# Sampled-state loads one group ahead, one gate tile forward, another tile order and new task delays in a hybrid decoder trunk

## The chip, the cores and the metric

The kernel runs on one core of one Trainium2 chip. TensorE (PE) multiplies, VectorE (DVE), ScalarE (ACT) and GpSimd (POOL) work element by element, and SyncE (SP) issues the transfers between the chip's memory and the core. The metric is the device time of one execution in microseconds (us), lower is better.

## The reference

One inference step of a trunk with two layers, for 512 prompt tokens (one new sequence) and 8 sampled sequences of 4 tokens each: 544 tokens in all, model width 1024. Layer 0 is a gated delta rule (GDN, 8 heads of 128), layer 1 a Mamba-2 scan (SSD, 32 heads of 64 in 4 groups, state size 128); each is followed by a SwiGLU FFN of width 2816, and every sublayer stands between two RMS norms. Of the SSD mixer, which most of the change touches:

```python
z, xBC, dt = jnp.split(h @ w_in, [SSD_DI, SSD_DI + SSD_CONV_DIM], axis=-1)
xBC, conv_new = causal_conv(xBC, conv0, conv_w, conv_b)
xs, Bm, Cm = jnp.split(jax.nn.silu(xBC), [SSD_DI, SSD_DI + SSD_GROUPS * SSD_DSTATE], axis=-1)
dt = jax.nn.softplus(dt + dt_bias)
y, hN = ssd_chunked(xs, dt, A, Bm, Cm, h0)     # h0: each sampled sequence's state
y = rms_norm((y + D_skip[:, None] * xs) * jax.nn.silu(z), norm_w)
return y @ w_out, hN, conv_new
```

In `ssd_chunked` each group multiplies its C by the state h0 of the sequence (`y_off`). In GDN the gate z enters at the end: the normed output of the delta rule is multiplied by silu(z), and the product goes through `gdn_w_out`.

## The kernel before

All data is feature-major: 128 features on the partitions, tokens along the row, in two halves of 272 tokens (hf 0 and 1). A weight block of 128 x 512 is loaded by SP (`wr`, 256 KB), split by ACT into a rounded high part (`wh`, L242) and by DVE into the rest (`wl`, L243), and for each 128 x 128 piece three matmuls are issued: high data by high weight (L279), low data by high weight (L280), high data by low weight (L281), each over 272 columns. The program has 11008 of these weight matmuls in its stages GDN mixer, GDN output projection, FFN 0, SSD mixer, SSD output projection, FFN 1. A place in the program is given below as @n: after the n-th weight matmul.

Everything else is done by small tasks, Python generators that a clock interleaves with the weight tiles (`Flow`, from L88). The clock counts one for each product of a weight piece. A task yields `(cost, delay)` or a condition, and is taken up again when the clock has gone on by the delay. The constants at the top (`D_...`, `PACE`, `NEWTON`, `TILE`, `FACTOR`) are such delays: `D_FIN` and `NEWTON` stand ahead of the two matmuls (`ms`, `r`) of a layer norm, `D_QT` ahead of the work on a tile of q, `PACE` between the state updates (`su`) that run beside the FFNs, `D_WT` ahead of the task that makes the decay matrices `W`. So the delays decide behind which weight matmul a small matmul stands. Each engine then works through its own queue in order; SP's is one queue for all loads and stores, and a DMA there waits until its buffer is free and until an earlier DMA on the same of eight semaphores has ended. What is behind it waits too.

The order of the tiles is written out. `ORDER` (L41) names the tiles of the GDN mixer, for each head k, q, v and z. In the SSD mixer a loop builds the order (L1681 to L1692): the dt tile, `NZ` gate tiles, B and C of group 0, then 16 x tiles, with B and C of the next group after every fourth, and from x3 on a gate tile behind each. `FINE` and `WIDE` say how many of the first tiles are emitted piece by piece and how many may use the larger set of PSUM banks. `T_S` is the number of tiles of the SSD output projection that are done for half 0 first and come again for half 1.

For each SSD group `c_task` (L1476) multiplies C and B (`cb`), then the states of the eight sampled sequences (`yos <- h0T, cm`, L1508, two at a time, b0 to b7), copies the sum from PSUM (L1514), transposes it (`yoT`, L1518). The states come as `h0T`, 256 KB each, in four buffers: b0 to b3 are loaded when the group's task starts, and b4 to b7 each when the matmul that read its buffer is through. `yos` on the SBUF side takes a buffer of the same four. A 128 x 32 by 128 x 512 matmul stands as two instructions in the trace, and one to four of them on different columns of the array take about the time of one.

The x tiles' task transposes x (`xtok`), multiplies the decay matrices W, which DVE makes from a broadcast row `ar` (loaded from memory, 272 KB) and CB, by x (`yd`), and makes the new state `hT`, which SP stores (`s_hp_out`).

Of the kernel before, what the change touches and what calls it, by code (L numbers as in the profile page):

```python
# [5 lines left out]
F32 = mybir.dt.float32  # L6
# [20 lines left out]
NL = 5  # L27
KEPT = 4
HELD = 3
NZ = 2  # L30
ZLAG = 3
SLEAD = 3
FINE = 12
WIDE = 4
NH0 = 4
PACE = 5.0
LIVE = 3
RAWW = 3 + SEQ + NB * 7

ORDER = ("k0 k1 z0 q0 q1 z1 k2 k3 v0 v1 z2 q2 q3 k4 k5 v2 v3 q4 q5 k6 k7 v4 v5 q6 q7 v6 v7 "  # L40
         "z3 z4 z5 z6 z7")  # L41
GLEAD = 3
FREE_G = (True, False)
FREE_S = (False, False)
NEWTON = 2.5
TILE = 1.0
FACTOR = 5.0
D_FIN = 2.5
D_DEC0 = 8.0
D_DEC1 = 3.5  # L50
D_DEC = 3.5
D_KT = 3.5
D_QT = 11.0
D_VT = 2.5
D_ON = 3.0
D_XT = 6.0
D_WT = 16.0
D_GT = 2.0
D_INV = 1.0
D_MG = 3.0  # L60
D_S1 = 0.8
D_S2 = 1.2
D_X3 = 3.0
# [1 line left out]
D_B0 = 0.0  # L65
T_G = 5
T_F = 4
T_S = 4
BIG = 1.0e30


# [45 lines left out]
def _program(nc, tc, io, es):  # L117
# [7 lines left out]
    act = pool("act", 6)  # L125
# [6 lines left out]
    def dma(out, in_):  # L132
        nc.sync.dma_start(out=out, in_=in_)
# [188 lines left out]
    def emit(u, fine=False, wide=False):  # L322
# [107 lines left out]
    class Pre:  # L430
# [18 lines left out]
        def end(self):  # L449
            if self.free:  # L450

                st.ready[self.hf] = True
                yield 0.0, FACTOR
            y = rsq(self.ss.sum(), 1e-6)
            yield 0.0, NEWTON
            r = spread(y)
            st.ready[self.hf] = True
            if self.free:
                st.r[self.hf] = sqp.tile([P, H2], F32, tag="sq", name="r", bufs=NSQ)
                S.activation(out=st.r[self.hf], in_=r, func=AF.Copy)  # L460
# [21 lines left out]
    class Post:  # L482


        def __init__(self, kind, layer, fw, e=1e-6, extra=None):
            self.kind, self.layer, self.fw, self.e, self.extra = kind, layer, fw, e, extra
            self.ss = [None, None]
            st.ready = [False, False]

        def tile(self, m):  # L490
            def done(hf, ps):
                if self.ss[hf] is None:
                    self.ss[hf] = Squares()
# [160 lines left out]
    def gdn():  # L654
# [697 lines left out]
    def ssd():  # L1352
# [118 lines left out]
        def c_after(m, Y):  # L1471
# [2 lines left out]
            S.activation(out=g.C, in_=Y, func=AF.Silu)  # L1474
            flow.start(c_task(m - 20), 6.0)

        def c_task(gi):
            g = gp[gi]
            h0 = []

            def load(n):
                for b in range(len(h0), min(n, NB)):
                    h0.append(big.tile([P, 512], F32, tag="h0T", name="h0T", bufs=NH0))
                    dma(h0[b], io["s_h0T"][b, :, 512 * gi:512 * gi + 512])
# [80 lines left out]
        def x_task(m, xf):  # L1565
# [107 lines left out]
        tiles += [zt(m) for m in range(NZ)] + [bt(0), ct(0)]  # L1673
        xs = {}
        z = NZ
        for m in range(16):
            tiles.append(xt_(m))
            xs[id(tiles[-1][0])] = m
            if m % 4 == 2 and m < 12:
                tiles += [bt(m // 4 + 1), ct(m // 4 + 1)]  # L1680
            if m >= ZLAG:  # L1681
                tiles.append(zt(z))
                z += 1
        tiles += [zt(m) for m in range(z, 16)]
        for i, u in enumerate(units(start_first(tiles, xop, SLEAD))):
# [12 lines left out]
        conv.close("s")
# [129 lines left out]
```

## Time and profile before

| | us |
|---|---|
| median of 3 runs | 1754.37 |
| the runs | 1745.22 to 1757.28 |
| the profiled execution | 1746.99 |
| its span in the trace | 1745.2 |
| TensorE busy | 1680.0 (96%) |
| VectorE busy | 1177.2 (67%) |
| ScalarE busy | 820.0 (47%) |
| GpSimd busy | 116.1 (7%) |

The profiled execution is 1.8 us longer than its span, and 7.4 us below the median. The mean granted clock of TensorE is 0.988 of its full 2.4 GHz. A row of the timeline gives start and duration of one instruction or of several of one kind in a row, the engine, the line, what it writes and reads, and behind it in brackets how long its engine stood idle before it and what ended that. Durations of matmuls overlap, so the time of a matmul is the distance from its start to the next start.

### The profile page before, as it was taken

Reading aid. Unit: us, or ns where it says so; the run is one execution under the profiler, and the core shown is the slowest. Engines: PE = TensorE matmul, PEld = TensorE weight load, DVE = VectorE, ACT = ScalarE, POOL = GpSimd, SP = SyncE. Lnnn points to the kernel's source line nnn. Section 1 sums busy time; section 2 is a strip of 40 time slices with the busy share of each in tenths; the row PEclk is TensorE's granted clock in tenths of the full one; section 3 lists DMA queues with packets and bytes.
Section 4 is the critical chain, followed back from the end, with each engine's and each line's share of the span. In section 5 each row is a group of like instructions: output and inputs, shape, how many; then the busy total and the mean of one; then the engine's idle time right before and its main releaser. Section 6 shows DMA issues by size and latency. Waiting matters only on the chain. (4 is left out here: it accounts for less than half of the span.)

```text
span 1745.2 us, 37143 instructions
## 1 busy us (share of the span) xinstructions
PE 1680.0 (96%) x14127; PEld 1597.6 (92%) x14127; DVE 1177.2 (67%) x3103; ACT 820.0 (47%) x1813; POOL 116.1 (7%) x335
## 2 busy tenths in 40 slices
PE   6899999999999999999699999999999999999997
PEld 5888888899999999999687899999999999999996
DVE  6886868567846665336877887878469766665356
ACT  5664644447433333335465565657456433333252
POOL 1212121100000000000001110100000000000000
PEclk8999999999999999999899999999999999999998
DMA  6333323335224443235544544432445644444464
GB/s 175 103 91 86 106 68 99 101 114 177 80 74 146 139 136 95 77 108 164 189 111 126 170 142 141 131 107 66 145 153 165 194 146 139 139 146 133 129 177 127
DMA packets 164563, 223.23 MB, mean 128 GB/s; under 512 B 53344, under 2 KB 66464, under 8 KB 163872
## 3 DMA queue, kind: packets, MB, share of 16 engines
q1 hardware_dynamic: 164384, 220.85, 41.9%
q8 instruction: 111, 1.82, 0.4%
q14 instruction: 68, 0.56, 0.1%
HBM read 199.75 MB, written 21.04 MB: 127 GB/s over the span
## 5 line engine op out<-in xcount | busy, mean ns | idle before, releaser
L279 PE MATMUL mm<-xh,wh 128*128 128x272 f32 x2496 | 735.7, 295 | 6.6 <-ACT og L1175 2.3
L280 PE MATMUL mm<-xl,wh 128*128 128x272 f32 x2496 | 727.7, 292 | 0.1
L281 PE MATMUL mm<-xh,wl 128*128 128x272 f32 x2496 | 727.1, 292 | 0.0
L242 ACT ACTIVATE wh<-wr 128x512 fp32r<-128x512 f32 x558 | 345.1, 622 | 408.3 <-PE mm L280 352.6
L243 DVE TENSOR_TENSOR wl<-wr,wh 128x512 fp32r<-128x512 f32 x558 | 376.5, 679 | 222.7 <-ACT wh L242 209.9
L279 PEld LDWEIGHTS mm<-xh,wh 128*128 128x128 f32 x2496 | 473.1, 190 | 23.9 <-issue 9.9
L280 PEld LDWEIGHTS mm<-xl,wh 128*128 128x128 f32 x2496 | 472.9, 190 | 4.7 <-issue 1.2
L281 PEld LDWEIGHTS mm<-xh,wl 128*128 128x128 f32 x2496 | 471.9, 189 | 4.8 <-issue 3.7
L279 PE MATMUL mm<-gb,wh 128*128 128x272 f32 x544 | 157.7, 291 | 0.0
L281 PE MATMUL mm<-gb,wl 128*128 128x272 f32 x544 | 155.5, 288 | 1.6 <-DVE wl L243 1.6
L280 PE MATMUL mm<-gb,wh 128*128 128x272 f32 x544 | 155.4, 288 | 0.0
L616 DVE SCALAR_TENSOR_TENSOR conv<-raw,cw,conv 128x512 f32<-128x512 f32 x144 | 107.0, 743 | 16.0 <-ACT conv L612 9.3
L281 PEld LDWEIGHTS mm<-gb,wl 128*128 128x128 f32 x544 | 101.8, 188 | 2.1 <-DVE wl L243 1.8
L279 PEld LDWEIGHTS mm<-gb,wh 128*128 128x128 f32 x544 | 102.2, 188 | 1.0 <-ACT wh L242 0.2
L280 PEld LDWEIGHTS mm<-gb,wh 128*128 128x128 f32 x544 | 102.3, 189 | 0.4
L1281 ACT ACTIVATE sg<-sg 128x272 f32<-128x272 f32 x88 | 37.6, 431 | 103.6 <-DVE sg L1280 103.3
L511 POOL TENSOR_TENSOR x<-x,fw 128x272 f32<-128x272 f32 x16 | 15.4, 964 | 1022.6 <-DVE fw L509 515.9
L280 PE MATMUL mm<-yl,wh 128*128 128x272 f32 x256 | 74.3, 291 | 1.2 <-DVE yl L359 1.2
L1289 DVE TENSOR_TENSOR sg<-sg,mm 128x272 f32<-128x272 f32 x88 | 38.4, 437 | 54.6 <-PE mm L281 54.3
L281 PE MATMUL mm<-yh,wl 128*128 128x272 f32 x256 | 73.9, 291 | 1.1 <-DVE wl L243 1.1
L279 PE MATMUL mm<-yh,wh 128*128 128x272 f32 x256 | 74.0, 290 | 0.0
L424 DVE TENSOR_TENSOR acc<-acc,sq 128x272 f32<-128x272 f32 x112 | 50.5, 454 | 33.2 <-ACT sq L417 32.6
(412 smaller groups left out, 2567.0 us busy)
## 6 DMA issues: line engine op xcount, KB each, us to landing
wr<-f_d_in SPq DMA_DIRECT2D x120, 256.0 KB
wr<-f_g_in SPq DMA_DIRECT2D x98, 256.0 KB
wr<-f_u_in SPq DMA_DIRECT2D x98, 256.0 KB
wr<-g_w_in SPq DMA_DIRECT2D x68, 256.0 KB
wr<-s_w_in SPq DMA_DIRECT2D x48, 256.0 KB
wr<-s_wo_in SPq DMA_DIRECT2D x48, 256.0 KB
wr<-s_wz_in SPq DMA_DIRECT2D x36, 256.0 KB
ar<-ad SPq DMA_DIRECT2D x32, 272.0 KB
```

The lines of the kernel that those rows point to most:

```text
L242: S.activation(out=hi, in_=src, func=AF.Copy)
L243: V.tensor_tensor(out=lo, in0=src, in1=hi.bitcast(F32), op=ALU.subtract)
L279: PE.matmul(ps, lhsT=h[:, k, :], rhs=ah(k0 + k), start=first and k == 0, stop=False)
L280: PE.matmul(ps, lhsT=h[:, k, :], rhs=al(k0 + k), start=False, stop=False)
L281: PE.matmul(ps, lhsT=lo[:, k, :], rhs=ah(k0 + k), start=False, stop=last and k == n - 1)
L424: V.tensor_tensor(out=self.acc, in0=self.acc, in1=self.late.pop(0), op=ALU.add)
L511: E.tensor_tensor(out=x[:, k, :], in0=x[:, k, :], in1=f, op=ALU.add)
L616: V.scalar_tensor_tensor(out=Y[:, 0:SEQ], in0=R[:, j:j + SEQ], scalar=w[:, j:j + 1], in1=Y[:, 0:SEQ], op0=ALU.mult, op1=ALU.add)
L1281: S.activation(out=t, in_=t, func=AF.Silu)
L1289: V.tensor_tensor(out=t, in0=t, in1=ps, op=ALU.mult)
```

## The change

1. SSD's tile order is written out as `SORDER`. z3 moves from behind x4 to behind x5, z4 from behind x5 to behind x7, z5 from in front of x7 to behind it, z6 and z7 come behind x8, z8 and z9 behind x9; z2 and everything from z10 on keep their places.
2. `c_task` loads a state b+5 behind the yield that follows b, no longer right behind its matmul, and at its end loads the first four states of the next group. The SBUF copy of `yos` leaves the four state buffers for a pool of 128 x 544 tiles, so the four are states alone.
3. The task of an x tile waits also for the group's `yo` (the transposed state product).
4. In GDN's `ORDER` z3 moves from behind v7 to behind q3.
5. Delays: `PACE` 5 to 6, `D_QT` 11 to 9.5, `D_DEC1` 3.5 to 2; `NEWTON`, `FACTOR`, `D_FIN` by stage; `FINE` 12 to 24, `WIDE` 4 to 8; `T_S` 4 to 5, by which four more blocks of the SSD output projection are loaded and split a second time (45 loads, before 41).
6. `emit_together` is new, but the tuples that would call it (`KO_G`, `KO_S`) are empty. Two `og` tiles are taken from their pool earlier in the loop.

```diff
-NZ = 2
-ZLAG = 3
-FINE = 12
-WIDE = 4
+FINE = 24
+WIDE = 8
-PACE = 5.0
+PACE = 6
...
-ORDER = ("k0 k1 z0 q0 q1 z1 k2 k3 v0 v1 z2 q2 q3 k4 k5 v2 v3 q4 q5 k6 k7 v4 v5 q6 q7 v6 v7 "
-         "z3 z4 z5 z6 z7")
+ORDER = ("k0 k1 z0 q0 q1 z1 k2 k3 v0 v1 z2 q2 q3 z3 k4 k5 v2 v3 q4 q5 k6 k7 v4 v5 q6 q7 v6 "
+         "v7 z4 z5 z6 z7")
+
+SORDER = ("z0 z1 B0 C0 x0 x1 x2 B1 C1 x3 z2 x4 x5 z3 x6 B2 C2 x7 z4 z5 x8 z6 z7 x9 z8 z9 "
+         "x10 B3 C3 x11 z10 x12 z11 x13 z12 x14 z13 x15 z14 z15")
...
-NEWTON = 2.5
-TILE = 1.0
-FACTOR = 5.0
-D_FIN = 2.5
+NEWTON = (2.5, 2.5, 1.5, 2.5, 3.2)
+TILE = (1.0, 1.0, 1.0, 1.0, 1.0)
+FACTOR = (5.0, 5.0, 5.0, 4, 5.0)
+D_FIN = (2.5, 2.5, 2.5, 2.5, 3.5)
...
-D_DEC1 = 3.5
+D_DEC1 = 2
...
-D_QT = 11.0
+D_QT = 9.5
...
-T_S = 4
+T_S = 5
...
+        def load_h0(gi, n):
+            h0 = gp[gi].h0
+            for b in range(len(h0), min(n, NB)):
+                h0.append(big.tile([P, 512], F32, tag="h0T", name="h0T", bufs=NH0))
+                dma(h0[b], io["s_h0T"][b, :, 512 * gi:512 * gi + 512])
+            return h0
...
-            load(NH0)
+            h0 = load_h0(gi, NH0)
...
-                    load(b + 1 + NH0)
                     if q % 2 and b < NB - 1:
-                        yield 1.7, 1.5
-            yo = big.tile([P, 512], F32, tag="h0T", name="yos", bufs=NH0)
+                        yield 1.7, D_Y
+
+                        load_h0(gi, b + 1 + NH0)
+            yo = t544("yos")[:, 0:512]
...
+            if gi < 3:
+                load_h0(gi + 1, NH0)
             yield 0.5, 0.5
...
-            yield lambda: hasattr(d, "w")
+            yield lambda: hasattr(d, "w") and hasattr(g, "yo")
```

The order on SP about the second half of group 0's states, before: the load of b4, one of b5, then b6 and b7, and further down, behind a store and several loads, the first four of group 1.

```order
L133 DMA h0T<-s_h0T_in 128x512
L133 DMA ar<-ad 128x544
L133 DMA h0T<-s_h0T_in 128x512
L133 DMA ar<-ad 128x544
L133 DMA ep<-ead 64x544
L133 DMA h0T<-s_h0T_in 128x512 x2
L133 DMA ep<-ead 64x544
L133 DMA wr<-s_w_in 128x512
L133 DMA wr<-s_wz_in 128x512
L133 DMA ar<-ad 128x544 x2
L133 DMA ep<-ead 64x544
L133 DMA s_hp_out<-hT 128x128
```

In the changed kernel, the same place:

```order
L137 DMA ar<-ad 128x544 x2
L137 DMA ep<-ead 64x544
L137 DMA h0T<-s_h0T_in 128x512 x2
L137 DMA ar<-ad 128x544
L137 DMA ep<-ead 64x544
L137 DMA h0T<-s_h0T_in 128x512
L137 DMA s_hp_out<-hT 128x128
L137 DMA h0T<-s_h0T_in 128x512 x2
L137 DMA ar<-ad 128x544
L137 DMA ep<-ead 64x544 x2
L137 DMA h0T<-s_h0T_in 128x512 x3
L137 DMA ar<-ad 128x544
```

b4 and b5 stand together, b6 alone, the store of `hT` now stands ahead of b7, and the four loads of group 1 (the one behind b7 and the row of three) follow at once, between the loads `ar` and `ep` of the x tiles.

The order on PE about group 1's states, before: one matmul on b4, the transposes of an x tile, one on b5; twelve weight matmuls earlier stand b0 to b3 in one row, and 24 later b6 and b7.

```order
L1508 MATMUL yos<-h0T,cm 32x512
L1571 MATMUL xtok<-cst,xf 128x128 x4
L1573 MATMUL xsm<-cst,xf 32x128
L1508 MATMUL yos<-h0T,cm 32x512
L279 MATMUL mm<-xh,wh 128x272
```

In the changed kernel b0 and b1 stand between the transposes and b2 and b3 behind them; twelve weight matmuls on follow b4 and b5, and b6 and b7 come behind the x tile's products, with no weight matmul between.

```order
L1615 MATMUL xtok<-cst,xf 128x128 x2
L1549 MATMUL yos<-h0T,cm 32x512 x2
L1615 MATMUL xtok<-cst,xf 128x128 x2
L1617 MATMUL xsm<-cst,xf 32x128
L1549 MATMUL yos<-h0T,cm 32x512 x2
L284 MATMUL mm<-xh,wh 128x272
```

```order
L1638 MATMUL su<-xw,Bt 128x128 x4
L1549 MATMUL yos<-h0T,cm 32x512 x2
L1661 MATMUL yd<-W,xt 64x128 x8
L1664 MATMUL yo<-W,xts 64x32 x2
L1666 MATMUL yo<-Cf,hT 128x128 x3
L1549 MATMUL yos<-h0T,cm 32x512 x2
L284 MATMUL mm<-xh,wh 128x272
```

The order on DVE in the square root that ends GDN's delta rule (`nx` to `ny`, then `dg`, which `r` on PE waits for). Before, three splits `kl` of FFN weights stand between its first steps:

```order
L368 TENSOR_SCALAR nx<-os 68x16
L243 TENSOR_TENSOR kl<-wr,kh 128x512
L369 TENSOR_SCALAR ny<-nx 68x16
L371 TENSOR_SCALAR nh<-nx 68x16
L243 TENSOR_TENSOR kl<-wr,kh 128x512
L372 TENSOR_TENSOR nt<-ny 68x16
L243 TENSOR_TENSOR kl<-wr,kh 128x512
L373 TENSOR_TENSOR nt<-nt,nx 68x16
```

In the changed kernel two of them stand ahead of it and one inside:

```order
L248 TENSOR_TENSOR kl<-wr,kh 128x512
L1170 TENSOR_TENSOR oar<-oss,qs_4652 128x272
L248 TENSOR_TENSOR kl<-wr,kh 128x512
L401 TENSOR_SCALAR nx<-os 68x16
L248 TENSOR_TENSOR kl<-wr,kh 128x512
L402 TENSOR_SCALAR ny<-nx 68x16
L404 TENSOR_SCALAR nh<-nx 68x16
L405 TENSOR_TENSOR nt<-ny 68x16
```

On PE the matmul `os` that this root waits for stands at @1587 before and at @1599 in the changed kernel, and `r`, which waits for the root, at @1624 in both.

## Rows read from the trace of the kernel before

**Rows 1.** The page, busy time by engine, and the three costliest groups of instructions (busy us, mean ns of one, idle time before and what ended most of it).

```profile
PE 1680.0 (96%) x14127; PEld 1597.6 (92%) x14127; DVE 1177.2 (67%) x3103; ACT 820.0 (47%) x1813; POOL 116.1 (7%) x335
...
L279 PE MATMUL mm<-xh,wh 128*128 128x272 f32 x2496 | 735.7, 295 | 6.6 <-ACT og L1175 2.3
L280 PE MATMUL mm<-xl,wh 128*128 128x272 f32 x2496 | 727.7, 292 | 0.1
```

**Rows 2.** What PE waited for over the whole span: us in total, times, longest.

```profile
PE ms L396 <- DVE acc L424: 11.9, 5, 8.4
PE r L388 <- DVE dg L385: 10.4, 6, 3.5
PE mm L288 <- DVE whl L243: 8.6, 1, 8.6
PE yos L1508 <- DMA h0T<-s_h0T_in: 3.8, 2, 2.1
PE mm L281 <- DVE wl L243: 2.7, 3, 1.6
...
PE c L1394 <- ACT Ac L1446: 1.4, 1, 1.4
PE mm L280 <- DVE yl L359: 1.2, 1, 1.2
```

**Rows 3.** The timeline of PE about group 0's states (start us, duration us).

```profile
913.12 0.29 PE L280 MATMUL mm<-xl,wh 128*128 128x272 f32 x1
913.24 0.29 PE L281 MATMUL mm<-xh,wl 128*128 128x272 f32 x1
913.46 1.05 PE L1508 MATMUL yos<-h0T,cm 128*32 128x512 f32 x4
914.44 1.16 PE L1594 MATMUL su<-xw,Bt 128*128 128x128 f32 x8
915.53 1.86 PE L1508 MATMUL yos<-h0T,cm 128*32 128x512 f32 x4
917.32 0.39 PE L279 MATMUL mm<-xh,wh 128*128 128x272 f32 x1
917.55 0.29 PE L280 MATMUL mm<-xl,wh 128*128 128x272 f32 x1
...
920.71 1.04 PE L1508 MATMUL yos<-h0T,cm 128*32 128x512 f32 x2 [1.75 <-DMA h0T<-s_h0T_in]
```

**Rows 4.** The same stretch, loads of PE's stationary operand: the wait inside the row that starts at 915.53.

```profile
916.34 0.14 PEld L1508 LDWEIGHTS yos<-h0T,cm 128*32 128x32 f32 x2 [0.68 <-DMA h0T<-s_h0T_in]
```

**Rows 5.** The timeline of PE about group 1's states.

```profile
967.45 1.06 PE L1508 MATMUL yos<-h0T,cm 128*32 128x512 f32 x8
972.29 1.04 PE L1508 MATMUL yos<-h0T,cm 128*32 128x512 f32 x2 [2.06 <-DMA h0T<-s_h0T_in]
```

**Rows 6.** Busy time by stretches of 1 us: PE, PEld, DVE, ACT, POOL, each with its instructions, then the granted clock of PE, the busy share of the DMA engines and GB/s.

```profile
922.00:923.00 1.00, 1.00 (x7) 0.75 (x6) 0.00 (x0) 0.00 (x0) 0.19 (x1) 0.59 0.74 236
923.00:924.00 1.00, 1.00 (x3) 0.14 (x2) 0.00 (x0) 0.00 (x0) 0.00 (x0) 0.50 0.52 188
924.00:925.00 1.00, 1.00 (x3) 0.20 (x2) 0.00 (x0) 0.09 (x1) 0.00 (x0) 0.50 0.86 244
925.00:926.00 1.00, 1.00 (x6) 1.00 (x7) 0.00 (x0) 1.00 (x2) 0.00 (x0) 0.70 0.96 246
...
973.00:974.00 1.00, 1.00 (x5) 0.73 (x5) 0.00 (x0) 0.00 (x0) 0.00 (x0) 0.69 0.78 277
974.00:975.00 1.00, 1.00 (x4) 0.23 (x3) 0.30 (x2) 0.60 (x1) 0.00 (x0) 0.50 0.96 227
975.00:976.00 1.00, 1.00 (x2) 0.00 (x0) 0.90 (x3) 0.00 (x0) 0.00 (x0) 0.50 0.77 230
976.00:977.00 1.00, 1.00 (x4) 0.70 (x4) 1.00 (x7) 0.00 (x0) 0.00 (x0) 0.60 0.95 313
```

**Rows 7.** The same view in a stretch of 5 us.

```profile
915.00:920.00 5.00, 3.97 (x21) 2.11 (x19) 4.59 (x15) 0.28 (x1) 0.34 (x2) 1.00 1.02 271
```

**Rows 8.** The timeline of SP: when the DMAs were issued.

```profile
910.70 0.38 SPq L133 DMA_DIRECT2D h0T<-s_h0T_in  x1
...
914.53 0.80 SPq L133 DMA_DIRECT2D h0T<-s_h0T_in  x2
...
921.61 0.34 SPq L133 DMA_DIRECT2D s_hp_out<-hT  x1
...
968.53 1.28 SPq L133 DMA_DIRECT2D h0T<-s_h0T_in  x3
```

**Rows 9.** The timeline of DVE behind group 0's states: decay matrices from `ar`, the idle time, and the first product of W and CB.

```profile
915.41 0.87 DVE L1544 TENSOR_SCALAR W<-ar,sGm 128x128 f32<-128x128 f32 x4 [1.47 <-DMA ar<-ad]
...
927.78 0.69 DVE L1577 TENSOR_TENSOR xw<-xtok,coef 128x512 f32<-128x512 f32 x1 [6.20 <-ACT xt L1575]
...
932.27 0.72 DVE L1553 TENSOR_TENSOR W<-W,CB 128x544 f32<-128x544 f32 x1
```

**Rows 10.** The end of GDN's delta rule, PE.

```profile
380.98 0.60 PE L1140 MATMUL os<-cst,oar 128*68 128x4 f32 x8
386.19 2.00 PE L388 MATMUL r<-dg,cst 68*128 68x272 f32 x8
```

**Rows 11.** The same, DVE.

```profile
381.62 0.17 DVE L368 TENSOR_SCALAR nx<-os 68x16 f32<-68x16 f32 x1
381.73 0.69 DVE L243 TENSOR_TENSOR kl<-wr,kh 128x512 fp32r<-128x512 f32 x1
...
385.21 1.49 DVE L385 TENSOR_TENSOR dg<-cst,ny 68x272 f32<-68x272 f32 x4
```

More of the change, by code (lines that the diff above doesn't have):

```diff
@@ L29 @@
 HELD = 3
-NZ = 2
-ZLAG = 3
 SLEAD = 3
-FINE = 12
-WIDE = 4
+FINE = 24
+WIDE = 8
 NH0 = 4
-PACE = 5.0
+PACE = 6
 LIVE = 3
 RAWW = 3 + SEQ + NB * 7
-ORDER = ("k0 k1 z0 q0 q1 z1 k2 k3 v0 v1 z2 q2 q3 k4 k5 v2 v3 q4 q5 k6 k7 v4 v5 q6 q7 v6 v7 "
-         "z3 z4 z5 z6 z7")
+ORDER = ("k0 k1 z0 q0 q1 z1 k2 k3 v0 v1 z2 q2 q3 z3 k4 k5 v2 v3 q4 q5 k6 k7 v4 v5 q6 q7 v6 "
+         "v7 z4 z5 z6 z7")
+SORDER = ("z0 z1 B0 C0 x0 x1 x2 B1 C1 x3 z2 x4 x5 z3 x6 B2 C2 x7 z4 z5 x8 z6 z7 x9 z8 z9 "
+         "x10 B3 C3 x11 z10 x12 z11 x13 z12 x14 z13 x15 z14 z15")
+KO_G = ()
+D_Y = 1.5
+KO_S = ()
 GLEAD = 3
@@ L44 @@
 FREE_S = (False, False)
-NEWTON = 2.5
-TILE = 1.0
-FACTOR = 5.0
-D_FIN = 2.5
+NEWTON = (2.5, 2.5, 1.5, 2.5, 3.2)
+TILE = (1.0, 1.0, 1.0, 1.0, 1.0)
+FACTOR = (5.0, 5.0, 5.0, 4, 5.0)
+D_FIN = (2.5, 2.5, 2.5, 2.5, 3.5)
 D_DEC0 = 8.0
-D_DEC1 = 3.5
+D_DEC1 = 2
 D_DEC = 3.5
 D_KT = 3.5
-D_QT = 11.0
+D_QT = 9.5
 D_VT = 2.5
-D_ON = 3.0
+D_ON = 3
 D_XT = 6.0
-D_WT = 16.0
+D_WT = 16
 D_GT = 2.0
-D_INV = 1.0
-D_MG = 3.0
+D_INV = 1
+D_MG = 3
 D_S1 = 0.8
@@ L211, in _program @@
     st.free = [False, False]
+    st.stage = 0
     st.held = [[], []]
@@ L347, in emit, with emit_together @@
         flow.product(us * (s.shape[1] if fine else k0))
+    def emit_together(us, wide=False):
+        for u in us:
+            fetch_to(u[4] + len(pieces(u[0])))
+        hf = us[0][1]
+        ah, al = us[0][2](hf)
+        banks = [mmt(wide) for _ in us]
+        for k in range(KD):
+            for (srcs, _, _, _, base, kept), ps in zip(us, banks):
+                one, end = k == 0, k == KD - 1
+                if srcs[0].shape[2] < P:
+                    w = ready[base][0]
+                    PE.matmul(ps[0:64], lhsT=w[:, k, :], rhs=ah(k), start=one, stop=False)
+                    PE.matmul(ps[0:64], lhsT=w[:, k, :], rhs=al(k), start=False, stop=end)
+                    continue
+                h, lo = ready[base + k // 4]
+                j = k % 4
+                PE.matmul(ps, lhsT=h[:, j, :], rhs=ah(k), start=one, stop=False)
+                PE.matmul(ps, lhsT=h[:, j, :], rhs=al(k), start=False, stop=False)
+                PE.matmul(ps, lhsT=lo[:, j, :], rhs=ah(k), start=False, stop=end)
+            flow.product(1.0)
+        for u, ps in zip(us, banks):
+            if st.free[hf] and st.r[hf] is None:
+                st.held[hf].append((u[3], ps))
+            else:
+                u[3](hf, ps)
+            flow.pump()
     def stack(tile, src, first):
@@ L452, in end @@
                 st.ready[self.hf] = True
-                yield 0.0, FACTOR
+                yield 0.0, FACTOR[st.stage]
             y = rsq(self.ss.sum(), 1e-6)
-            yield 0.0, NEWTON
+            yield 0.0, NEWTON[st.stage]
             r = spread(y)
@@ L488, in __init__ @@
             st.ready = [False, False]
+            st.stage += 1
         def tile(self, m):
@@ L497, in done @@
                 if self.ss[hf].n == KD:
-                    flow.start(self.finish(hf), D_FIN)
+                    flow.start(self.finish(hf), D_FIN[st.stage])
             return done
@@ L502, in finish @@
             y = rsq(self.ss[hf].sum(), self.e, None if self.extra is None else self.extra[:, half(hf)])
-            yield 0.0, NEWTON
+            yield 0.0, NEWTON[st.stage]
             r = spread(y)
@@ L512, in finish @@
                 pre.square(k)
-                yield 0.0, TILE
+                yield 0.0, TILE[st.stage]
             yield from pre.end()
@@ L1207, in gdn @@
             n = names.get(id(u[0]))
-            if i == 1:
+            if i == 1 or (i == 0 and 0 in KO_G):
                 load_small()
+            if i == 2:
+                og += [act.tile([P, 4, T], F32, tag="x", name="og") for _ in range(2)]
             if i == 2 * GLEAD - 1:
@@ L1213, in gdn @@
                 load_zeros()
-                og += [act.tile([P, 4, T], F32, tag="x", name="og") for _ in range(2)]
             if n is not None and u[1] == 0 and i >= GLEAD and n[0] == "k":
@@ L1220, in gdn @@
                     flow.start(decay(h // 2 + 1), D_DEC)
+            if i % GLEAD < 3 and i < 2 * GLEAD and i // GLEAD in KO_G:
+                if i % GLEAD == 0:
+                    emit_together(us[i:i + 3])
+                continue
             emit(u)
@@ L1451, in ssd @@
         pr = [State() for _ in range(16)]
+        for g in gp:
+            g.h0 = []
         def b_after(m, Y):
@@ L1475, in c_after @@
             flow.start(c_task(m - 20), 6.0)
+        def load_h0(gi, n):
[4 more added lines that the diff above has]
+            return h0
         def c_task(gi):
             g = gp[gi]
[L1479 to L1484, printed above, removed]
-            load(NH0)
+            h0 = load_h0(gi, NH0)
             ps = dbank("cb")
@@ L1672, in ssd @@
         zt = lambda m: ([io["s_wz"][m]], z_done(m))
-        tiles += [zt(m) for m in range(NZ)] + [bt(0), ct(0)]
         xs = {}
[L1675 to L1685, printed above, removed]
+        for n in SORDER.split():
+            i = int(n[1:])
+            tiles.append({"x": xt_, "z": zt, "B": bt, "C": ct}[n[0]](i))
+            if n[0] == "x":
+                xs[id(tiles[-1][0])] = i
+        us = units(start_first(tiles, xop, SLEAD))
+        for i, u in enumerate(us):
             flow.until(lambda: st.ready[u[1]])
@@ L1695, in ssd @@
                     flow.start(w_task(m + 2), D_WT)
+            if i < 2 * SLEAD and i % SLEAD < 3 and i // SLEAD in KO_S:
+                if i % SLEAD == 0:
+                    emit_together(us[i:i + 3], True)
+                continue
             emit(u, i < FINE, i < WIDE)
```

## The prediction

> **What bounds the kernel now.** I began with the page: TensorE is busy for 1680.0 of 1745.2 us, and nearly all of it is the three weight matmuls of a piece [rows 1]. A busy PE with spare time on every other engine leaves three things to gain: the 65 us in which PE is idle, the time in which it is busy at half clock, and small matmuls in between. The change keeps the number of weight matmuls and of small ones, so only these three can move. Next I read what ended PE's idle time [rows 2]. The largest entries, `ms`, `r` and `whl`, are the start of the program, the end of it and the norms between layers. I compared the order of both kernels there: where FFN 0 passes into SSD, at the longest wait of 8.4 us, PE and DVE have the same instructions in the same order up to the `r` that ends it, so this stays. What the change does touch is the entry `yos <- h0T`, 3.8 us in two waits.
>
> The timelines show what these cost. In group 0 PE waits 1.75 us at 920.71 for the state b6 [rows 3]; inside the row that starts at 915.53 there is a third wait, 0.68 us, for b5 [rows 4]. In group 1 it waits 2.06 us at 972.29 for b4 [rows 5]. The view by microseconds shows a second cost that no list of waits has: behind either wait the granted clock falls from the upper level (2.4 GHz) to the lower (1.2 GHz). What is missing from full clock between 922 and 926 is 0.41 + 0.50 + 0.50 + 0.30 = 1.71 us, between 973 and 977 it is 0.31 + 0.50 + 0.50 + 0.40 = 1.71 us [rows 6]. So group 0's late loads cost 0.68 + 1.75 + 1.71 = 4.14 us and group 1's 2.06 + 1.71 = 3.77 us, together 7.9 us. That is the most that the loads can give.
>
> **The loads, step by step.** b5 was issued at 910.70 and landed at 916.34, after 5.6 us; b6 was issued at 914.53 and used at 920.71, after 6.2 us; group 1's b4 was issued at 968.53 and used at 972.29, after 3.8 us [rows 3 to 5, 8]. I take 3.8 to 6.2 us for a load in this stretch.
>
> Group 0: by the orders, the matmul that frees b6's buffer moves ahead, from @5440 to @5428, and its use back, from @5451 to @5463. Between stand 35 weight matmuls, at 0.125 us from start to start (913.12 to 913.24 [rows 3]) 4.4 us, a `su` of 1.1 us and the `yos` of b4 and b5 with 1.0 us [rows 3], in all 6.5 us and some tenths for the passages between shapes. Two short DMAs go ahead of b6 on SP, about 1 us. So b6 waits between 0 and 0.7 us. b7 now stands behind the store of `hT` on SP. That store was issued at 921.61 [rows 8], far too late, but in the new order the `su` that it needs stands 8 weight matmuls earlier, and on DVE no weight split and no convolution is left between it and `hT`; I work out 916.7 on the old clock. b7 would land between 921 and 923 and is used near 922: a wait of 0 to 1.3 us. Of 4.14 us I leave 0.7 us, gain 3.4 us.
>
> Group 1: its b0 to b3 are now loaded near 917 to 922 and used some 45 us later, no question. Its b4 and b5 are still loaded after b0 and b1 were used, the change doesn't prefetch those. From there to their use are the rest of the transposes, one `yos`, twelve weight matmuls and a `su`: 0.5 + 1.0 + 1.5 + 1.1 us and passages, 4.1 to 4.5 us, against 3.8 us for the load of that very place. A wait of 0 to 0.5 us (up to 2.0 if 6.2 us held here). I leave 0.4 us, gain 3.4 us.
>
> Together the loads give 6.8 us of 7.9; the other end, nothing, is a rival below.
>
> [...]
>
> **Passages between shapes.** From a weight matmul to a small one and back costs 0.22 - 0.125 at the way in (913.24 to 913.46) and 0.23 - 0.125 at the way out (917.32 to 917.55), 0.2 us [rows 3]. Counting runs of small matmuls in both orders, GDN has 153 instead of 157 and SSD 68 instead of 77: with the others 12 fewer. Bounds 0 (a passage between two small shapes costs as much) and 2.4 us; I take 1.2 us.
>
> **z3 in GDN's tail.** One tile, 48 weight matmuls, 6.1 us, no longer covers the end of the delta rule. There `os` starts at 380.98 and `r` at 386.19 [rows 10], with 37 weight matmuls between, and the root on DVE takes 3.6 us from `nx` to `dg` [rows 11]. Now 25 lie between, 3.2 us. But two of three weight splits, 0.69 us each [rows 11], stand ahead of the root instead of inside it, which shortens it by about 1 us. Add 0.6 us from `os` to `nx` [rows 10, 11]: `dg` is ready about 3.6 us behind `os`, PE comes there after 3.7. The steps before it stand only 1 and 4 weight matmuls apart and may wait 0.3 us each. Bounds 0 and 6.1 us, all cover exposed; I take +0.6 us, near the lower end since the root is worked out from its own rows.
>
> **Edits at nothing.** `T_S` adds four loads and splits beside the SSD projection, where ACT and DVE are half idle (47% and 67% [rows 1]); its cover is that spare time, and without it each split would cost 0.7 us. Beside the norms' shifted delays there stands a wait of 1.2 us for `yl` [rows 2] that stays. The head of SSD (`FINE`, `WIDE`) has a wait of 1.4 us for `Ac` [rows 2] whose chain comes some 23 weight matmuls later while its user does too: -1 to +1.5 us. The later `su` tasks of FFN 1 end ahead of the last norm. `D_QT` moves single waits of 1 to 2 us: -2 to +2 us.
>
> Sum: -6.8 - 1.2 + 0.6 = -7.4 us on the profiled 1746.99, or 1739.6 us. The median of the runs stands 7.4 us above that execution; against it I forecast 1754.37 - 7.4 = **1747 us**.
>
> **Rivals.** (1) *The loads stay late.* For it: the second half of each group is still loaded only after the first was used, and b7 has moved behind a store that ran at 921.61 [rows 8]. Then one wait and its half clock stay in each group, about 3.5 us each, and the loads give 1 us instead of 6.8: 1754.4 - 1.0 - 1.2 + 0.6 = 1753 us. Against it: b6's distance grows by 12 + 12 weight matmuls.
>
> (2) *The burst holds back the decay matrices: slower.* The four loads of group 1, 1 MB, go out between 917 and 922, ahead of `ar` loads in the same queue, while the DMA engines are at share 1.02 and 271 GB/s [rows 7]; they take 3.9 us of it. DVE makes W from that `ar`, and in its order the row now stands ahead of the product of W and CB that `yd` needs; before it had 6.20 us of idle time there, and the product came at 932.27 [rows 9]. `yd` moves ahead from @5508 to @5488, 2.5 us. If `ar` lands as late as 926, the product comes near 929 and PE, there at about 926, waits 3 us and then loses 1.7 us of clock. With b7 held back by the same traffic, 4 us with its clock, group 0 costs 8.7 instead of 4.1 us, group 1 gains 3.4: +1.2, less 1.2, plus 0.6, plus up to 2 us if the next `ar` is late too: 1755 to 1757 us. It decides from `ar` landing later than about 924. By the rows above I get 922 to 924. [...]
>
> (3) *More is won.* If b6, b7 and b4 never wait, the passages give 2.4 us, and a wait of GDN or the head goes with its half clock (2 to 4 us), the sum is -12 to -15 us: 1740 us.
>
> **Chances.** Forecast 0.52 (1743 to 1750 us), rival 1 0.22, rival 2 0.12, rival 3 0.14. Runs of one kernel spread from 1745.22 to 1757.28, so a median of few moves by some 4 us by itself. The range that leaves out 2 in 10, with the bounds of GDN's tail: 1736 to 1757 us. This kernel's measurement tells 1%, 17.5 us, from no change. Beyond it on the fast side lies the tail of rival 3, 0.08; on the slow side almost nothing, 0.02; within 0.90.
>
> **What would show it.** In the new trace: no wait of `yos` over 1 us in groups 0 and 1, and the granted clock at 1.00 behind them; `ms <- acc` still 8.4 us; `r <- dg` near 383 under 0.5 us; `yd` without a wait for W. I am wrong if `yos` still stands among the waits with 2 us or more, or if GDN's stage is longer by more than 2 us.

## The result, and the profile after

| | us |
|---|---|
| before, median of 12 runs | 1752.67 (1742.19 to 1763.72) |
| after, median of 12 runs | 1739.72 (1737.09 to 1746.34) |
| ratio, 95% interval | 0.9938 [0.9916, 0.9961] |
| profiled execution of after, its span | 1744.72, 1742.9 |
| TensorE, VectorE, ScalarE, GpSimd busy | 1683.4 (97%), 1180.8 (68%), 821.4 (47%), 110.2 (6%) |

The changed kernel is faster by 0.6%, 10.9 us by the ratio (the medians lie 13.0 us apart). Forecast were 1747 us and 7.4 us. The time lies in the range of 1736 to 1757 us, but below the 1743 to 1750 us that I had called the forecast, where rival 3 stands; the change is below the 1% that was set as the bound. Most of the reasons didn't come out, as the experiments show. Two runs beside the last four experiments, one of before and one of e12, took 3.2 ms at a granted clock of 1.00 and stand outside all medians, ratios and means below.

The page of after, busy time and the three weight matmuls, against [rows 1]:

```profile
PE 1683.4 (97%) x14127; PEld 1602.6 (92%) x14127; DVE 1180.8 (68%) x3107; ACT 821.4 (47%) x1816; POOL 110.2 (6%) x335
...
L284 PE MATMUL mm<-xh,wh 128*128 128x272 f32 x2496 | 735.4, 295 | 5.9 <-ACT og L1209 2.3
L286 PE MATMUL mm<-xh,wl 128*128 128x272 f32 x2496 | 728.3, 292 | 1.3 <-DVE wl L248 1.2
L285 PE MATMUL mm<-xl,wh 128*128 128x272 f32 x2496 | 728.7, 292 | 0.0
```

What PE waited for in after, against [rows 2] (us in total, times, longest):

```profile
PE ms L429 <- DVE acc L457: 12.8, 6, 8.4
PE r L421 <- DVE dg L418: 10.9, 6, 3.5
PE mm L293 <- DVE whl L248: 8.2, 1, 8.2
PE mm L286 <- DVE wl L248: 3.8, 4, 1.6
...
PE sk L1133 <- DMA S<-g_S_in: 1.3, 2, 0.9
```

The entry `yos <- h0T`, 3.8 us before, is gone, and `ms` still has its 8.4 us. Behind group 0's states and group 1's the clock stays at its upper level (5-us windows, columns as in [rows 6, 7]); before, it fell there to the lower one [rows 6]:

```profile
915.00:920.00 5.00, 5.00 (x37) 3.98 (x35) 4.40 (x20) 2.52 (x6) 0.00 (x0) 1.00 0.92 246
920.00:925.00 5.00, 5.00 (x29) 3.05 (x28) 4.11 (x14) 1.70 (x5) 0.87 (x5) 1.00 0.58 171
...
970.00:975.00 5.00, 5.00 (x35) 2.99 (x34) 3.65 (x15) 2.31 (x5) 0.00 (x0) 1.00 0.62 209
```

So the step that I had put first happened as described. But the two traces, laid side by side by the n-th weight matmul, add up badly: from @5000 to @5740 (SSD's first groups) after needs 153.2 us instead of 161.6, and in GDN (@0 to @1680) 391.1 instead of 387.0. The second number meets the condition under which I had called myself wrong, GDN longer by more than 2 us. What made it longer stands in the same view, in GDN:

```profile
115.00:120.00 5.00, 3.48 (x167) 2.98 (x166) 2.60 (x12) 2.17 (x9) 0.57 (x3) 1.00 0.50 118
120.00:125.00 5.00, 5.00 (x89) 4.26 (x88) 3.68 (x11) 1.37 (x4) 2.37 (x6) 0.61 0.44 77
125.00:130.00 5.00, 5.00 (x40) 4.50 (x38) 2.23 (x11) 2.55 (x6) 0.69 (x3) 0.50 0.04 5
130.00:135.00 5.00, 5.00 (x34) 4.50 (x33) 0.76 (x4) 1.37 (x3) 0.32 (x1) 0.50 0.25 79
135.00:140.00 5.00, 5.00 (x32) 4.68 (x32) 3.79 (x19) 1.42 (x4) 0.00 (x0) 0.69 0.61 190
```

Behind a stretch of dense tiny matmuls (`mg`, 32x32: 167 matmuls in 5 us) TensorE ran at 1.2 GHz: of these windows (0.39 + 0.50 + 0.50 + 0.31) x 5 = 8.5 us are missing from full clock. With the falls near 30 and 80 us, half clock lasts 27.3 us in after's GDN and 10.2 us in before's; take half of each away, and GDN needs 377.5 us in after and 381.9 in before. Before's profiled execution has the same matmuls at the same place at 1.00:

```profile
115.00:120.00 5.00, 4.05 (x170) 3.54 (x169) 2.82 (x12) 2.43 (x11) 0.57 (x3) 1.00 0.46 115
120.00:125.00 5.00, 5.00 (x107) 4.32 (x106) 4.67 (x17) 2.65 (x8) 2.40 (x6) 1.00 0.39 75
```

Either trace is one draw. So from here on I read three things of each kernel: the median; each run's time split into what its clock cost, (1 - granted clock) x span, and the rest, called T0, its time at full clock; and two stretches of its trace. Of the clock loss and T0 only differences between kernels are used, for half clock counts as lost even where PE stands idle, as at the end of before:

```profile
1740.00:1745.00 5.00, 0.00 (x0) 0.00 (x0) 2.05 (x6) 0.00 (x0) 0.76 (x1) 0.50 0.49 167
```

### The profile page after: what moved, and what is told of

It is laid out like the page before. It is cut to its first block, busy times and chain, and to the rows that moved or that the text cites. A ratio compares the mean times of both kernels' runs of the same rounds, so it can differ in the third digit from the quotient of the medians.

```text
span 1742.9 us, 37139 instructions
## 1 busy us (share of the span) xinstructions
PE 1683.4 (97%) x14127; PEld 1602.6 (92%) x14127; DVE 1180.8 (68%) x3107; ACT 821.4 (47%) x1816; POOL 110.2 (6%) x335
## 5 line engine op out<-in xcount | busy, mean ns | idle before, releaser
L247 ACT ACTIVATE wh<-wr 128x512 fp32r<-128x512 f32 (+1 forms) x562 | 347.5, 622 | 415.9 <-PE mm L285 366.5
L248 DVE TENSOR_TENSOR wl<-wr,wh 128x512 fp32r<-128x512 f32 (+1 forms) x562 | 379.9, 680 | 217.4 <-ACT wh L247 199.5
L284 PE MATMUL mm<-gb,wh 128*128 128x272 f32 x544 | 157.4, 291 | 0.0
L286 PE MATMUL mm<-gb,wl 128*128 128x272 f32 x544 | 155.6, 288 | 1.6 <-DVE wl L248 1.6
L1319 DVE TENSOR_TENSOR sg<-mm,r 128x272 f32<-128x272 f32 x88 | 38.6, 441 | 60.9 <-PE mm L286 58.6
```

Of the source, the lines that this page charges most:

```text
L247: S.activation(out=hi, in_=src, func=AF.Copy)
L248: V.tensor_tensor(out=lo, in0=src, in1=hi.bitcast(F32), op=ALU.subtract)
L284: PE.matmul(ps, lhsT=h[:, k, :], rhs=ah(k0 + k), start=first and k == 0, stop=False)
L286: PE.matmul(ps, lhsT=lo[:, k, :], rhs=ah(k0 + k), start=False, stop=last and k == n - 1)
L1319: V.tensor_tensor(out=t, in0=ps, in1=st.r[hf], op=ALU.mult)
```

## The experiments

The first four runs ask which half of the change pays, the next four which part of each half, the last four why. Times are us; T0 and clock loss are means over the runs; the two stretches are from each kernel's one traced execution.

| kernel | median | ratio to before, 95% | T0 | clock loss | GDN, @0 to @1680 | SSD, @5000 to @5740 |
|---|---|---|---|---|---|---|
| before, beside e1 to e4 | 1751.18 | | 1725.5 | 25.7 | 387.0 | 161.6 |
| before, beside e5 to e8 | 1748.67 | | 1725.9 | 23.3 | | |
| before, beside e9 to e12 | 1748.71 | | 1726.8 | 24.4 | | |
| after | 1739.72 | 0.9938 [0.9916, 0.9961] | 1719.6 | 21.3 | 391.1 | 153.2 |
| e1 loads alone | 1751.36 | 1.0012 [0.9983, 1.0041] | 1727.1 | 26.4 | 392.5 | 159.0 |
| e2 after, loads back | 1742.03 | 0.9963 [0.9938, 0.9988] | 1722.5 | 21.5 | 381.6 | 158.2 |
| e3 GDN part alone | 1740.27 | 0.9951 [0.9931, 0.9972] | 1720.9 | 20.3 | 383.5 | 157.4 |
| e4 after, GDN part back | 1751.21 | 1.0003 [0.9973, 1.0034] | 1723.1 | 27.4 | 393.8 | 154.3 |
| e5 z3 alone | 1741.93 | 0.9961 [0.9942, 0.9980] | 1722.3 | 20.5 | 382.3 | 157.7 |
| e6 GDN's delays alone | 1750.26 | 1.0014 [0.9987, 1.0041] | 1726.3 | 24.7 | 392.0 | 157.8 |
| e7 SSD part alone | 1747.52 | 0.9994 [0.9976, 1.0012] | 1723.2 | 25.5 | 387.6 | 155.7 |
| e8 SSD's order alone | 1748.86 | 1.0000 [0.9977, 1.0022] | 1726.2 | 24.1 | 390.7 | 157.7 |
| e9 before, less `mg` late | 1738.71 | 0.9940 [0.9906, 0.9975] | 1719.7 | 21.9 | 379.5 | 157.9 |
| e10 after, less `mg` first | 1742.18 | 0.9955 [0.9920, 0.9989] | 1720.0 | 23.1 | 382.6 | 154.5 |
| e11 after, z4 forward too | 1746.09 | 0.9960 [0.9927, 0.9994] | 1719.8 | 24.9 | 391.4 | 155.6 |
| e12 GDN and SSD parts | 1742.05 | 0.9937 [0.9905, 0.9970] | 1720.3 | 22.3 | 383.9 | 154.0 |

T0 varies little between the runs of a kernel (standard deviation 1.2 to 1.6 us, so some 0.4 us on a mean of 12), although their times spread over 9 to 25 us: nearly all of the spread is clock.

**e1**, the loads alone, on before:

```diff
-            load(NH0)
+            h0 = load_h0(gi, NH0)
...
-                    load(b + 1 + NH0)
                     if q % 2 and b < NB - 1:
                         yield 1.7, 1.5
-            yo = big.tile([P, 512], F32, tag="h0T", name="yos", bufs=NH0)
+
+                        load_h0(gi, b + 1 + NH0)
+            yo = t544("yos")[:, 0:512]
...
+            if gi < 3:
+                load_h0(gi + 1, NH0)
...
-            yield lambda: hasattr(d, "w")
+            yield lambda: hasattr(d, "w") and hasattr(g, "yo")
```

> The kernel before with the change's load order of the sampled states alone (four loads a group ahead, b4 to b7 behind the yield, the copy of yos in another pool, the x task waiting for yo), the tile order and the delays as before. Theory: the late loads and the half clock behind them are the main cost, 7.9 us, and the loads alone give most of it: 5 to 8 us faster (ratio 0.9955 to 0.997), no wait of yos over 1 us in groups 0 and 1, the granted clock 1.00 from 915 to 985. Rival (the order of the tiles is what spaced the loads): under 2 us faster, a wait of yos of 1 us or more left.

Measured: nothing won, 1.0012, and a T0 above before's by 1.6 us. Two waits for states stay:

```profile
PE yos L1510 <- DMA h0T<-s_h0T_in: 2.6, 2, 1.7
```

In the old tile order the prefetch doesn't come in time. Behind these waits the clock stays at 1.00 in the traced execution. What adds the 1.6 us of T0 was not looked into.

**e2**, the changed kernel with these lines as before.

> The changed kernel with the loads of the states as before, the rest of the change kept. Theory: it loses what the loads gave, 5 to 8 us against the changed kernel (about 1746 us where the changed one is at 1740), and the waits of yos with their half clock come back in groups 0 and 1. Rival (tile order): it keeps nearly the whole gain, within 2 us of the changed kernel.

Measured: 2.3 us above after in the median, 2.9 us in T0. In its trace no `yos` waits, but the decay matrices are late instead, and behind them the clock falls in the window from 925 to 930 us:

```profile
PE yd L1656 <- DVE W L1592: 1.9, 1, 1.9
```

```profile
925.00:930.00 5.00, 5.00 (x34) 4.11 (x33) 2.74 (x8) 1.56 (x4) 1.30 (x3) 0.66 0.03 7
```

In the new order the loads are worth 2 to 3 us, and in this trace not by the wait that I had read, but by another in its place.

**e3**, only the GDN part, on before:

```diff
-ORDER = ("k0 k1 z0 q0 q1 z1 k2 k3 v0 v1 z2 q2 q3 k4 k5 v2 v3 q4 q5 k6 k7 v4 v5 q6 q7 v6 v7 "
-         "z3 z4 z5 z6 z7")
+ORDER = ("k0 k1 z0 q0 q1 z1 k2 k3 v0 v1 z2 q2 q3 z3 k4 k5 v2 v3 q4 q5 k6 k7 v4 v5 q6 q7 v6 "
+         "v7 z4 z5 z6 z7")
-D_DEC1 = 3.5
+D_DEC1 = 2
-D_QT = 11.0
+D_QT = 9.5
```

> The kernel before with GDN's part alone: z3 forward in the order, D_QT 9.5, D_DEC1 2. Theory of the prediction: GDN as a whole moves by -1 to +2 us. Rival from the changed kernel's trace: single waits in GDN (vtok, qk, sk, mg) fall from 6.0 to 2.3 us, so 3 to 5 us faster where the clock stays up, and a stretch of half clock near 122 to 139 us, worth 8 us, comes in some executions and not in others.

Measured: 1740.27 us, as fast as the whole change within the intervals. What I had priced at +0.6 us is most of the gain. T0 falls by 4.6 us. Where that comes from stands in PE's waits between 100 and 380 us. Before:

```profile
PE mg L913 <- issue: 2.4, 2, 1.5
PE qk L975 <- ACT qT L960: 1.5, 1, 1.5
PE sk L1099 <- POOL Dt L917: 1.1, 1, 1.1
PE vtok L1013 <- ACT vT L1003: 1.1, 1, 1.1
PE mg L927 <- issue: 0.7, 1, 0.7
PE mm L279 <- DVE raw L474: 0.2, 1, 0.2
```

and e3:

```profile
PE mg L913 <- issue: 1.0, 1, 1.0
PE mm L279 <- DVE raw L474: 0.5, 2, 0.3
PE sk L1099 <- DMA S<-g_S_in: 0.4, 1, 0.4
PE mg L927 <- DVE Y L914: 0.4, 1, 0.4
PE mm L279 <- ACT conv L612: 0.2, 1, 0.2
```

7.0 us of waits became 2.5, and the 4.5 us between them are about as large as T0's 4.6. One execution of each is a draw here too: the same sum is 5.7 to 7.0 us (mean 6.4) in the six traces with the old order and all the work (before, e1, e4, e6, e7, e8) and 2.2 to 4.1 us (mean 2.9) in the five with z3 alone forward (after, e2, e3, e5, e12). That is 3.5 us, the lower end of what T0 shows. In before they are small waits of the delta rule's chains, for the transposed q (`qT`), the transposed v (`vT`), the decay terms (`Dt`) and ahead of `mg`, at 119, 165, 208, 222, 252 and 321 us. z3's 48 weight matmuls, from the mixer's end, now stand in the midst of this work.

e3 also corrects the reading of SSD, since its SSD code is that of before. Its states about group 0:

```profile
911.80 1.80 PE L1508 MATMUL yos<-h0T,cm 128*32 128x512 f32 x4
916.13 1.05 PE L1508 MATMUL yos<-h0T,cm 128*32 128x512 f32 x2 [0.95 <-DMA h0T<-s_h0T_in]
```

and its windows there:

```profile
915.00:920.00 5.00, 4.05 (x19) 2.04 (x18) 2.74 (x13) 0.86 (x2) 0.54 (x3) 1.00 0.92 278
920.00:925.00 5.00, 5.00 (x44) 4.97 (x43) 3.33 (x14) 4.45 (x7) 0.19 (x1) 1.00 0.48 145
```

The late state is there too, with 0.95 us instead of 1.75, and the clock behind it stays at 1.00.

**e4**, the changed kernel with GDN's order and delays as before.

> The changed kernel with GDN's part undone (order of the tiles, D_QT, D_DEC1 as before). If GDN's part gives 3 to 5 us, this is 3 to 5 us slower than the changed kernel, about 1744 us where that is at 1740, and 7 to 9 us faster than the kernel before; if GDN's part gives nothing, it stands at the changed kernel's time.

Measured: 1.0003, the whole gain is gone, which neither reading had; T0 is 3.5 us above after's, inside the 3 to 5 us expected, but the clock loss is 6.1 us higher as well. `qk <- qT` 1.5 us, `vtok <- vT` 1.1 and `mg` 2.6 are back among its waits, and near 320 us the lower clock:

```profile
320.00:325.00 5.00, 4.11 (x63) 3.63 (x63) 1.73 (x3) 1.38 (x3) 2.73 (x6) 0.78 0.13 40
325.00:330.00 5.00, 5.00 (x57) 4.42 (x52) 0.35 (x1) 2.03 (x5) 0.00 (x0) 0.50 0.10 32
330.00:335.00 5.00, 5.00 (x37) 4.63 (x37) 2.19 (x4) 1.71 (x5) 0.34 (x2) 0.50 0.13 29
335.00:340.00 5.00, 5.00 (x25) 4.02 (x24) 1.07 (x4) 1.96 (x4) 0.00 (x0) 0.52 0.88 293
```

(0.22 + 0.50 + 0.50 + 0.48) x 5 = 8.5 us, again behind a stretch of `mg`.

**e5**, e3's `ORDER` alone, and **e6**, e3's two delays alone.

> The kernel before with only the order of GDN's tiles changed: z3 from behind v7 to behind q3. Theory after the first four runs: this one edit carries GDN's gain, since it moves the weight matmuls of a whole tile ahead of the third and fourth stretch of small mg matmuls. Then it is 7 to 11 us faster (ratio 0.994 to 0.996), PE's waits for vtok, sk and mg are shorter by 2 to 4 us, and the mean share of half clock falls by about 5 us. Rival (the delays D_QT and D_DEC1 carry it): within 2 us of the kernel before.

> The kernel before with D_QT 9.5 and D_DEC1 2 alone, z3 where it was. Theory (z3 carries the gain): within 2 us of the kernel before. Rival (the delays carry it): 5 us faster or more, the wait of 1.5 us for qT gone.

Measured: e5 0.9961, T0 -3.6 us, clock loss -2.8; e6 1.0014, T0 +0.4. In e6 the waits for `qT` and `vT` stand as before, and `mg` with 2.1 and 1.2 us:

```profile
PE qk L975 <- ACT qT L960: 1.5, 1, 1.5
PE vtok L1013 <- ACT vT L1003: 1.1, 1, 1.1
```

The moved tile pays, the delays by themselves don't; beside the tile they may add T0's last 1.0 to 1.4 us (e3 against e5), which is near what such means can tell. By the ratio e5's gain is 6.8 us, at the lower end of what was expected, and its clock loss falls by less than the 5 us. e6's trace has the lower clock at 250 us:

```profile
250.00:255.00 5.00, 3.79 (x77) 3.01 (x77) 0.35 (x1) 2.14 (x10) 2.93 (x7) 0.84 0.16 59
255.00:260.00 5.00, 5.00 (x52) 4.57 (x47) 2.75 (x6) 2.19 (x7) 1.36 (x4) 0.50 0.05 13
```

**e7**, the SSD part on before: e1's lines, `FINE`, `WIDE` and the tile order. **e8**, the tile order alone:

```diff
+SORDER = ("z0 z1 B0 C0 x0 x1 x2 B1 C1 x3 z2 x4 x5 z3 x6 B2 C2 x7 z4 z5 x8 z6 z7 x9 z8 z9 "
+         "x10 B3 C3 x11 z10 x12 z11 x13 z12 x14 z13 x15 z14 z15")
...
-        for m in range(16):
-            tiles.append(xt_(m))
...
+        for n in SORDER.split():
+            i = int(n[1:])
+            tiles.append({"x": xt_, "z": zt, "B": bt, "C": ct}[n[0]](i))
```

> The kernel before with all of SSD's mixer as changed (the loads, the tile order, FINE 24, WIDE 8) and GDN as before. Theory: loads and tile order together give 2 to 4 us, since the loads alone gave nothing in the old order and cost 2.3 us when taken out of the new one; yos has no wait. Rival (the loads are worth the 7.9 us of the prediction once the order fits): 6 to 8 us faster.

> The kernel before with SSD's new tile order alone, the loads as before. Theory (order and loads help only together): within 1.5 us of the kernel before, late loads left in the waits of yos. Rival (the order is what helps): 2 to 4 us faster.

Measured: e8 nothing (1.0000; its waits for states are 3.4 us). e7 has no such wait, and T0 falls by 2.7 us, but the ratio is 0.9994 and can't be told from 1. The loads need the order and the order the loads; together they are worth the stretch's 3 us. The last column of the table says this better than any pair of traces: four executions with the old SSD code (e3, e5, e6, e9) need 157.4 to 157.9 us, three with one half of it (e1, e2, e8) 157.7 to 159.0, six with the new one (after, e4, e7, e10, e11, e12) 153.2 to 155.7. Before's own profiled execution, on which the prediction stood, needs 161.6.

**e9**, one multiplication step of the delta rule's inverse left out for the last two pairs of heads, on before; **e10**, the same for the first pair, on the changed kernel (`if p > 0`):

```diff
-            ps = bank("mg").rearrange("p (e t c i) -> p e t c i", e=2, t=2, c=NC)
-            for e, c in ec:
...
+            if p < 2:
+                ps = bank("mg").rearrange("p (e t c i) -> p e t c i", e=2, t=2, c=NC)
+                for e, c in ec:
...
```

> The kernel before without the 64 small matmuls (32 x 32) and the subtraction of one Newton step in the third and fourth pair of heads: that part of the inverse is left out, so the output is not the reference's. Theory: the half clock that z3 forward makes rarer comes in behind these two dense stretches of small matmuls with PE's idle time in them. Then the microseconds lost to the clock fall by 3 to 5 on the mean of the runs (from about 24.5 to 20), like with z3 forward, and the rest falls by 2 to 5 us (the stretches themselves and their idle time): 5 to 9 us faster. Rival (the clock falls elsewhere, behind the waits for qT and vT): the time lost to the clock stays at 24 to 26 us, and the kernel is 2 to 5 us faster.

> The changed kernel without the same 64 small matmuls and subtraction in the first pair of heads alone (output not the reference's). Theory: the only stretch that still drops the clock in some executions is the first, near 120 us; then the slower executions (1741 to 1746 us) go away, the spread of the runs is under 5 us and the median falls by 2 to 5 us to about 1736. Rival (the spread of the runs is from elsewhere): the spread stays at 9 us, the median falls by 1 to 2 us.

Measured: e9's T0 falls by 7.1 us, the left-out work with it, and the clock loss by 2.5 us in the mean, where 2 to 5 and 3 to 5 were expected; its trace has no half clock in GDN behind the first 38 us. But four of its runs lie at 1747 to 1758 us, so the loss is made rarer at most. e10's clock loss, 23.1 us, is not below after's 21.3, and its runs spread over 17.9 us where under 5 were expected: a miss. That the step's matmuls set whether the clock falls is supported by the one and not by the other.

**e11**, one more tile forward, on the changed kernel:

```diff
-ORDER = ("k0 k1 z0 q0 q1 z1 k2 k3 v0 v1 z2 q2 q3 z3 k4 k5 v2 v3 q4 q5 k6 k7 v4 v5 q6 q7 v6 "
-         "v7 z4 z5 z6 z7")
+ORDER = ("k0 k1 z0 q0 q1 z1 k2 k3 v0 v1 z2 q2 q3 z3 k4 k5 v2 v3 q4 q5 z4 k6 k7 v4 v5 q6 q7 v6 "
+         "v7 z5 z6 z7")
```

> The changed kernel with z4 moved forward as well, from the end of GDN to behind q5, so that three gate tiles are left there. If the middle of GDN still lacks work to cover its small matmuls, it gains 1 to 3 us more; the prediction's worry, cover lost at the end of the delta rule, would show here as a wait of r for dg or of sc near 385 us of 2 us or more, and then it is 1 to 4 us slower than the changed kernel. Expected: the second, slower by 0 to 3 us.

Measured: T0 1719.8 against 1719.6, so a second tile fills nothing more; the median is 6.4 us higher by a clock loss of 24.9 us, its runs lie between 1736.33 and 1757.39, and the intervals overlap. The wait of `r` or `sc` near 385 us, the sign of lost cover, is not in its trace; a wait of 1.6 us for `mg` stands at 340 us. No gain, and whether it is slower stays open.

**e12**, GDN's and SSD's parts on before, without the new `PACE`, `NEWTON`, `FACTOR`, `D_FIN`, `T_S` and the `og` tiles:

```diff
-NEWTON = (2.5, 2.5, 1.5, 2.5, 3.2)
+NEWTON = 2.5
...
-T_S = 5
+T_S = 4
```

> The kernel before with GDN's part and SSD's mixer as changed, and the rest (PACE, NEWTON, FACTOR, D_FIN by stage, T_S, the og tiles) as before. Theory: the rest is worth nothing, so this stands within 1.5 us of the changed kernel. Rival: T_S and the delays around the norms give 2 us or more, and this is that much slower.

Measured: 0.9937, as after, T0 1720.3; the median is 2.3 us above after's, more than the 1.5 us expected, but by the ratios nothing lies between them. The rest is worth nothing that can be measured. No version with all of the work is surely faster than the changed kernel.

## Why the prediction was right or wrong

**The sum.** At full clock after is 5.9 to 7.2 us below before (1719.6 against 1725.5 to 1726.8), of which the GDN part gives 3.5 to 4.6 (e4, e3) and the SSD part 2.7 to 2.9 (e7, e2). The clock loss falls by another 2 to 4 us. I had 7.4 us, by other terms: -6.8 for the loads, -1.2 for passages, +0.6 for z3. That the sum came near is luck: some 5 us too much for SSD and 4 to 5 us too little for GDN cancel.

**The loads: mechanism right, size wrong.** The waits went, the clock behind the states stands at 1.00, and `yd` doesn't wait, as forecast. But of the 6.8 us, with the passages 8.0, the stretch gave 3.1 (157.7 to 154.6 us in the means of the executions named above). From before's own execution to after's it fell by 8.4 us, so the reading fits that one execution. The step that failed is "behind either wait the granted clock falls": 3.42 us read from two places of one execution [rows 6] were taken as a cost that each execution pays. e3, e5, e6 and e9, with the same SSD code, have the late states and no fall behind them, and shorter waits (2.1 to 2.9 us instead of 3.8). e1 and e8, with half of the new code, have none either. I had also taken the loads as a term of their own; e1 and e8 show that each half of the pair is worth nothing alone. The passages can't be told apart in this.

**z3: the tail right, the place it went to not looked at.** For the tail I had `dg` ready 3.6 us behind `os` and PE there after 3.7, and no wait above 0.5. In after it came so, `r` 3.68 us behind `os` without a wait:

```profile
386.17 0.60 PE L1174 MATMUL os<-cst,oar 128*68 128x4 f32 x8
389.85 2.08 PE L421 MATMUL r<-dg,cst 68*128 68x272 f32 x8
```

(Near 390 us, since the half clock above had put the stage back; in e3, without that, `r` stands at 382.19.) What failed is that the step priced only the cover that z3 leaves, and not what it covers where it arrives. The waits it removes were in the list that I argued from, `mg` with 2.4 us and `qk` with 1.5, above the 1.4 and 1.2 us that I did price [rows 2], and I had put them with `D_QT`, "single waits of 1 to 2 us". e6 shows that the delays don't move those for `qT`, `vT` and `mg`, e5 that the tile does.

**The clock in GDN: not in the prediction.** With the old GDN order (before, e1, e4, e6, e7, e8; 164 runs) the mean clock loss is 24.9 us, with z3 forward (after, e2, e3, e5, e11, e12; 71 runs) 21.8, less by 3.1 us with a 95% interval of 1.6 to either side. Of the traced executions with the old order, e1, e4, e6 and e8 lose 3.4, 8.5, 6.9 and 6.8 us to half clock behind the `mg` stretches near 250 or 320 us; before, e7 and e9 lose nothing there. With z3 forward none of seven does at these two places; only near 120 us, ahead of z3's new place, after, e11 and for a shorter time e12 do, as does e1 of the old order. So the moved tile goes with a rarer fall of the clock, by the runs and by the traces. At the same two places stand waits ahead of `mg`, in the six old-order traces 0.5 to 1.2 us near 252 and 0.9 to 1.5 us near 322; with z3 alone forward 0.3 to 0.4 us are left at the first and none at the second. But before and e7 have these waits without a fall. Why the fall is rarer, whether by the waits that z3 fills or by how the matmuls stand there, isn't settled by e9 and e10 and stays open.

**The clock, beside a page.** The Trainium skill, "TensorE: Matmul & The Clock Gate", in its part on the clock gate, says that how long a kernel runs slow at its start varies from run to run by the gate's phase, and that for modelling this costs less than 1% of a span. No run here can show that start, for the record of the clock begins some 20 us into the span. What the runs show is something else: falls later in the kernel that also differ from run to run, by which the whole span has a granted clock of 0.976 to 0.991, and (1 - granted clock) x span is 16 to 42 us.

**Edits at nothing.** Right: e12, without `T_S` and the delays around the norms, measures as after, and `D_QT` by itself gives nothing (e6). The reason had a slip, since a VectorE busy for 67% isn't half idle. `FINE` and `WIDE` weren't tried apart from the rest of e7.

**The rivals.** Rival 1 (loads stay late) is what e1 shows, in the old order only. Rival 2 (the burst holds back the decay matrices) fell: after's `yd` doesn't wait, and the late W comes in e2, where the prefetch is missing. Rival 3 (1740 us, "a wait of GDN goes with its half clock") had the measured time and, in that half sentence, the larger part of the mechanism; I gave it 0.14, as I had looked only at how the change could lose in GDN. Its terms add up to -11.7 to -14.3 us, not to -15.

## What to carry to other kernels

Read a stall that shows in one profiled execution, and above all a fall of the clock behind it, as a draw: compare its stretch in executions of kernels that share the code, and split each run's time into clock loss and the rest, which here told 3 us apart where the intervals of the ratios are 6 to 12 us wide. When a tile of filler moves, price what it covers at its new place as carefully as what it uncovers at the old one: add up the small waits of that stretch, even those too short for the top of the list. Two edits can be worth something only together; undo each from the changed kernel and do each alone.

## What the hardware showed beside this

On one core, with nothing else changed, runs of one kernel differ by 9 to 25 us, and almost all of that is TensorE's granted clock. In the traces the falls to 1.2 GHz last 3 to 17 us. Three of them stand in every one of the 14 traces: near 30 us, about the wait of 8.4 us for `acc` near 860 us, and in the last 10 to 13 us. The others that are shown above stand behind dense runs of 32x32 matmuls or short waits, and come in some executions and not in others with the same instructions (115 to 140 us in before and in after).
